# Three small moves in a one-core trunk layer: where one row of weights is loaded, which buffers hold the gate values, which PSUM bank holds the context state

## The chip, the cores and the metric

The kernel runs on one core of a Trainium2 chip. The metric is the device time of one execution in microseconds (us). Engines are named as the profile names them: PE is TensorE (PEld its weight load), DVE is VectorE, ACT is ScalarE, POOL is GpSimd, SP is SyncE, which here only issues DMAs. A q behind a name (ACTq, SPq) is that engine's instruction queue, whose instructions run in order.

## The reference, cut to what matters

One trunk layer over 512 latent tokens of width 1024, with a 256-token context prefix, in float32:

```
h    = rms_norm(x)*(1+scale)+shift ;  proj = h @ w_in
xbc  = silu(depthwise_conv4(proj[x,B,C]))                    # 8 groups of 4 heads
h0   = final SSD state of the context, forward and backward   # context only
y    = ssd_scan(forward, h0_f) + rev(ssd_scan(backward, h0_b)) + d_skip*xs
       # per 128-token chunk: y_diag + (C . state entering the chunk) * exp(la)
ssm  = group_rms_norm(y * silu(z)) @ w_out_ssm
conf = (silu(layer_norm(conv31(glu))) * silu(proj[cg])) @ w_out_conf
out  = (sigmoid(g1)*ssm + sigmoid(g2)*conf) @ w_out
x    = rms_norm(x + gate*out) * final_norm_w
```

## The kernel before, in words

Every big product is done in three float32r passes (high part by high part, high by low, low by high), 128 columns of weights at a time. A weight block of 128 x 1024 comes by DMA into `raw` (two buffers, on the SP queue), ACT copies it to `whi` (L168), DVE subtracts to get `wlo` (L169), and PE uses both; `whi` and `wlo` have three buffers each.

The order of the instructions on each engine is not the order of the program text. A planner sorts them: on each engine it takes, of the instructions whose inputs and buffers are free by its own estimate, the one that stands first in the program (`high_priority` ones, such as L168, L169 and `evac`, ahead). The engines then run this fixed order, and wait on semaphores where the real times differ from the estimates.

The stages that the change touches:

- **Eight groups** (L462 on). Per group: projections, conv, then the context state: two products into `cp` (L539), which ACT copies to `s0` (`evac`, L174). Then three state sums for the chunks, each a pair of products into a `cp` tile (L547), which DVE adds to the decayed state before it (L549, L551). `s0` and the three sums are the states entering the chunks; the carried-over outputs are products of these states with `cT` into `yo` (L586). All `cp` tiles take turns with the transposes and `sps` in the two banks of tag `m`; `yo` takes two banks of its own, one tile at a time. The order of the tiles in `m` is: context `cp`, first, second, third chunk's `cp`, then `sps`. With two banks, the second chunk's `cp` takes the bank of the context `cp`, and the third chunk's that of the first. The `yo` tile of a group is read by DVE (L591) before the next group begins.
- **The SSM output product** (L706 on, eight steps d of 48 matmuls). In steps 2 to 5 of the program text, two channel blocks k a step are turned into the conformer's input: transposes, a SiLU (L725), the product with the stored gate values `zcl` (L720 loads them from DRAM on the ACT queue, L726 multiplies), and the split into `vhi` and `vlo`. `zcl` has one buffer, tag `cr`. DVE also adds up the residual gate from `mg` blocks (L703), which go through `raw` like the weights. The result of step d is stored to DRAM on the ACT queue (L730).
- **The last products** (pool `fp`, L739 on). For each d: the conformer output product (24 matmuls, blocks `wc` on the SP queue), and the preparation of one block of `w_out`: it is loaded on the ACT queue into `rawo` (L146, two buffers), multiplied by the gate (L750), and split into `wh` and `wl`. DVE merges the two branches into `mg` (L761, L762, with `t2` and `m1b` loaded on the ACT queue), which is split into `mhi` and `mlo`. Then the last product (L777) runs over all d. `fnb`, the final norm's weights spread over 128 partitions (512 KB written), is loaded ahead of this loop on the ACT queue (L745) and first read at L780.

The pool `fp` lies where the pools `lnp` and `yp` lay. In bytes of a partition from their common start: `lnp` takes 16,896, `yhi` and `ylo` 32,768 each, so `t1` lies at 82,432 to 98,816, the two `gt` buffers (with `sv`) behind it to 102,912, and then `up`. In `fp`, `wh`, `wl`, `mhi` and `mlo` take 98,304, so `fnb` lies at 98,304 to 102,400 and the first `rawo` buffer at 102,400 to 106,496. So `fnb` overlaps the end of `t1`, whose last block is read by the last store of L730; `rawo` doesn't, it overlaps `gt` and `up`. A tile waits only for the tiles under it.

Of the kernel before, what the change touches and what calls it, by code (L numbers as in the profile page):

```python
# [8 lines left out]
F32 = mybir.dt.float32  # L9
# [6 lines left out]
P = 128  # L16
D = 1024
KO = D // P
L = 512
# [3 lines left out]
R = 4  # L23
# [57 lines left out]
def hybrid_block(ctx: ExitStack, tc: tile.TileContext, x, cx, pack, wmod, bgate, wall, fnw, out):  # L81
    nc = tc.nc
# [15 lines left out]
    def pv(name):  # L98
        o, w = OFF[name]
        return pk[:, o:o + w]  # L100
# [34 lines left out]
    def follow(ins, prev):  # L135
        tc.add_manual_dep(ins.ins, prev.ins.name,
                          mybir.DependencyInfo(mybir.DependencyClass.NoSync, mybir.DependencyReason.DATA),
                          reason="activation table order")
# [37 lines left out]
    def split(dst_hi, dst_lo, src):  # L176
        S.copy(dst_hi, src)
        V.tensor_sub(dst_lo, src, dst_hi.bitcast(F32))

    def log_exp_table(after):  # L180
        t = S.preload_act_table_set("natural_log_exp_and_others")
        follow(t, after)
        return t
# [107 lines left out]
    def acc_tile():  # L291
        pxn[0] += 1
        tag = pxt[pxn[0] % len(pxt)]
        return pp.tile([P, L], F32, name="px", tag=tag, bufs=2 if tag == "px" else 1)
# [60 lines left out]
    if True:  # L355
        pp_stack = ctx
        pp = pp_stack.enter_context(tc.tile_pool(name="pp", bufs=1, space=PSUM, reuse_waits="tile"))
# [65 lines left out]
        with tc.tile_pool(name="sp", bufs=1, reuse_waits="tile") as sp:  # L423
# [38 lines left out]
            for g in range(NG):  # L462
# [70 lines left out]
                        wend[:, d0:d1, c, h0:h0 + R].unsqueeze(3).broadcast_to([P, nd, R, 64]))  # L533
                    return w
                sts = []
                cp = pp.tile([P, 2, R, 64], F32, name="cp", tag="m", bufs=2)
                for i in range(NCC):
                    w = xw(NCH + i, 0, 2)
                    T.matmul(cp, btok[:, NCH + i], w, start=(i == 0), stop=(i == NCC - 1))  # L539
# [3 lines left out]
                for i in range(NCH - 1):  # L543
                    cp = pp.tile([P, 2, R, 64], F32, name="cp", tag="m", bufs=2)
# [29 lines left out]
                for t in range(2):  # L574
                    yd = pp.tile([P, L], F32, name="yd", tag="yd", bufs=1)
                    for c in range(NCH):
                        for hf in range(2):
                            r = 2 * t + hf
                            T.matmul(yd[hf * 64:(hf + 1) * 64, c * P:(c + 1) * P],  # L579
                                     xtok[:, c, t, hf * 64:(hf + 1) * 64], mixes[c][:, r], start=True, stop=True)  # L580
                    yo = pp.tile([P, 2, L], F32, name="yo", tag="yo", bufs=1)
# [33 lines left out]
        yp = ypool_stack.enter_context(tc.tile_pool(name="yp", bufs=1, reuse_waits="tile"))  # L615
# [3 lines left out]
        def gemm3(ps, d, rhi, rlo, between):  # L619
            i = 0  # L620
            for kind in ("ws0", "ws1"):
                hi, lo = wblock(kind, d)
                for k in range(KO):
                    T.matmul(ps, hi[:, k, :], rhi[:, i], start=(i == 0), stop=False)  # L624
                    T.matmul(ps, hi[:, k, :], rlo[:, i], start=False, stop=False)  # L625
                    T.matmul(ps, lo[:, k, :], rhi[:, i], start=False, stop=(i == 2 * KO - 1))  # L626
                    i += 1
                if kind == "ws0":
                    between()
# [5 lines left out]
        def to_tokens_all():  # L635
            while ready:
                to_tokens(*ready.pop(0))
# [12 lines left out]
        for i in range(KO - ne):  # L650
            up, _ = conv_in(yp, pp, ne + i)
            taps.append(conv_taps(yp, ne + i, up, lambda d, a: ready.append((d, a))))
            if i == 0:
# [6 lines left out]
                    for g in range(NG):  # L660
                        rb = yp.tile([P, L], F32, name="rb", tag="rb", bufs=2)
                        nc.scalar.dma_start(out=rb, in_=rs_d[g].rearrange("c l -> (c l)").unsqueeze(0).broadcast_to([P, L]))
                        for t in range(2):
                            jj = 2 * g + t
                            yl = yp.tile([P, L], F32, name="yl", tag="yl", bufs=2)
# [3 lines left out]
            for k in (2 * i, 2 * i + 1):  # L669
                pg, _ = proj(pp, "cg", k)  # L670
                zc = yp.tile([P, L], F32, name="zc", tag="gt", bufs=GT[0])
# [12 lines left out]
            if i < ne:  # L684
                cr = yp.tile([P, L], F32, name="cr", tag="cr", bufs=1)
# [15 lines left out]
        def gate(i):  # L701
            raw = wraw("mg", i)
            V.scalar_tensor_tensor(out=ga.rearrange("p n c -> p (n c)"), in0=raw, scalar=scg[:, i:i + 1],  # L703
                                   in1=ga.rearrange("p n c -> p (n c)"), op0=ALU.mult, op1=ALU.add)

        for d in range(KO):  # L706
            po = pp.tile([P, 2, L], F32, name="po", tag="yo", bufs=1)[:, 0] if d % 2 else pp.tile([P, L], F32, name="po", tag="yd", bufs=1)
            gemm3(po, d, yhi, ylo, lambda: gate(d))
            if d == 0:
                to_tokens_all()  # L710
                mv = yp.tile([P, NCH, 2], F32, name="mv")
                for t in range(NCH):
                    V.bn_aggr(out=mv[:, t], in_=bst[:, t])
                rl = rsqrt_small(yp, "rl", mv[:, :, 1], 1.0)
                for t in range(NCH):
                    V.tensor_scalar(ln[:, t], ln[:, t], mv[:, t, 0:1], rl[:, t:t + 1], op0=ALU.subtract, op1=ALU.mult)
            if 2 <= d <= 5:
                for k in (2 * d - 4, 2 * d - 3):
                    zc = yp.tile([P, L], F32, name="zcl", tag="cr", bufs=1)
                    nc.scalar.dma_start(out=zc, in_=cg_d[k])  # L720
                    tp = pp.tile([P, NCH, P], F32, name="tpb", tag="m", bufs=2)
                    for t in range(NCH):
                        T.transpose(tp[:, t], ln[:, t, k * P:(k + 1) * P], ident)
                    sv = yp.tile([P, L], F32, name="sv", tag="gt", bufs=GT[0])
                    last = S.activation(sv, tp.rearrange("p t c -> p (t c)"), AF.Silu, scale=pv("lnw")[:, k:k + 1], bias=pv("lnb")[:, k:k + 1])  # L725
                    V.tensor_mul(sv, sv, zc)  # L726
                    split(vhi[:, k], vlo[:, k], sv)
            with tc.high_priority():
                V.scalar_tensor_tensor(out=t1[:, d], in0=t1[:, d], scalar=1.0, in1=po, op0=ALU.add, op1=ALU.mult)
            nc.scalar.dma_start(out=m1d[d], in_=t1[:, d])  # L730
# [8 lines left out]
    with tc.tile_pool(name="fp", bufs=1, reuse_waits="tile") as fp:  # L739
        wh = fp.tile([P, KO, D], F32R, name="wh")  # L740
        wl = fp.tile([P, KO, D], F32R, name="wl")
        mhi = fp.tile([P, KO, L], F32R, name="mhi")
        mlo = fp.tile([P, KO, L], F32R, name="mlo")
        fnb = fp.tile([P, D], F32, name="fnb")
        nc.scalar.dma_start(out=fnb, in_=fnw.broadcast_to([P, D]))  # L745
        for d in range(KO):
            po = acc_tile()
            hi, lo = wblock("wc", d)
            raw = wraw("wo", d, fp, "rawo", 2, nc.scalar)
            V.tensor_mul(raw, raw, gb.rearrange("p n c -> p (n c)"))  # L750
            split(wh[:, d], wl[:, d], raw)
            for k in range(KO):
                T.matmul(po, hi[:, k, :], vhi[:, k], start=(k == 0), stop=False)
                T.matmul(po, hi[:, k, :], vlo[:, k], start=False, stop=False)
                T.matmul(po, lo[:, k, :], vhi[:, k], start=False, stop=(k == KO - 1))
            t2 = fp.tile([P, L], F32, name="t2", tag="t2", bufs=2)
            nc.scalar.dma_start(out=t2, in_=t2d[d])
            m1 = fp.tile([P, L], F32, name="m1b", tag="m1b", bufs=1)
            nc.scalar.dma_start(out=m1, in_=m1d[d])
            mg = t2  # L760
            V.scalar_tensor_tensor(out=mg, in0=t2, scalar=1.0, in1=po, op0=ALU.add, op1=ALU.mult)  # L761
            V.tensor_add(mg, mg, m1)  # L762
            split(mhi[:, d], mlo[:, d], mg)
        table = log_exp_table(last)
        for t in range(NCH):
            cs = slice(t * P, (t + 1) * P)
            xr = fp.tile([P, D], F32, name="xr", tag="xr", bufs=1)
            nc.scalar.dma_start(out=xr, in_=x[cs, :])
            o = fp.tile([P, D], F32, name="o", tag="o", bufs=2)
            parts = ((0, 512), (512, 512)) if t < NCH - 1 else ((0, 512), (512, 256), (768, 256))  # L770
            s2 = fp.tile([P, 3], F32, name="s2", tag="s2", bufs=2)[:, 0:len(parts)]
            for n, (c0, cn) in enumerate(parts):
                ns = slice(c0, c0 + cn)
                po = acc_tile()[:, 0:cn]
                for k in range(KO):
                    for st_, rh, a, b in ((mhi, wh, True, False), (mhi, wl, False, False), (mlo, wh, False, True)):
                        T.matmul(po, st_[:, k, cs], rh[:, k, ns], start=(a and k == 0), stop=(b and k == KO - 1))  # L777
                V.tensor_add(o[:, ns], po, xr[:, ns])
                S.activation(xr[:, ns], o[:, ns], AF.Square, accum_out=s2[:, n:n + 1])
                V.tensor_mul(o[:, ns], o[:, ns], fnb[:, ns])  # L780
            sm = fp.tile([P, 1], F32, name="sm", tag="sm", bufs=2)
            V.tensor_reduce(sm, s2, axis=mybir.AxisListType.X, op=ALU.add)
            r = rsqrt_small(fp, "rf", sm, 1.0 / D, table)
            S.mul(o[:, 0:512], o[:, 0:512], r)
            nc.sync.dma_start(out=out[cs, 0:512], in_=o[:, 0:512])
            V.tensor_scalar(o[:, 512:D], o[:, 512:D], r, None, op0=ALU.mult)
            nc.scalar.dma_start(out=out[cs, 512:D], in_=o[:, 512:D])
# [75 lines left out]
```

## Time and profile before

| | |
|---|---|
| time, three runs | 945.36 us median (943.8 to 948.3) |
| time of the profiled execution | 943.96 us |
| its span, first to last instruction | 941.9 us (2.06 us lie around it) |
| PE busy | 911.8 us, 97% of the span |
| DVE busy, ACT busy | 734.2 us (78%), 522.8 us (56%) |
| granted TensorE clock, mean | 0.995 |

Busy time is the time in which an engine has an instruction under way. Matmuls overlap, so two of them start some 0.23 us apart though each lasts 0.39. The time that counts is what is lost between the starts of PE's matmuls.

### The profile page before, as it was taken

What the parts mean: (1) busy time and instruction counts of PE and PEld (TensorE: products, weight loads), DVE (VectorE), ACT (ScalarE), POOL (GpSimd) and SP (SyncE); (2) the same over time, 40 slices, a digit from 0 to 9 for tenths busy, and PEclk for the clock granted to TensorE, in tenths of its full rate; (3) what the DMA queues carried; (4) which work ended last, traced back from release to release, by engine and by line L of the source; (5) the groups of instructions that cost most, each with busy time, mean ns of one, the idle gap of its engine ahead of it and who ended that gap; (6) DMA issues with size and microseconds to landing.
All of it is one profiled execution on the core that took longest, in us unless ns stands there. A gap on an engine that the chain in (4) does not pass through costs nothing.

```text
span 941.9 us, 12605 instructions
## 1 busy us (share of the span) xinstructions
PE 911.8 (97%) x4647; PEld 730.7 (78%) x4647; DVE 734.2 (78%) x1232; ACT 522.8 (56%) x926; POOL 10.1 (1%) x117
## 2 busy tenths in 40 slices
PE   6999999999999999999999999999999999999896
PEld 1287788788788788787887887788888888868686
DVE  1577499997699994899993999889999965448833
ACT  4638846767667668468477567454433234323322
POOL 0000000000000000000000000000000000000000
PEclk9999999999999999999999999999999999999999
DMA  9424512522422324225125122356633356568522
GB/s 378 193 87 140 180 45 84 173 58 97 149 68 98 119 92 158 73 68 180 44 90 179 34 79 79 131 204 215 212 112 132 114 179 205 152 180 267 190 78 79
DMA packets 41375, 127.04 MB, mean 135 GB/s; under 512 B 4546, under 2 KB 4962, under 8 KB 40291
## 3 DMA queue, kind: packets, MB, share of 16 engines
q1 hardware_dynamic: 25040, 93.22, 29.8%
q10 hardware_dynamic: 16274, 33.04, 10.3%
q8 instruction: 36, 0.59, 0.3%
q14 instruction: 25, 0.20, 0.1%
HBM read 112.46 MB, written 13.78 MB: 134 GB/s over the span
## 4 chain that ended last, share of the span: by engine, by line
PE 71%; ACT 11%; DMA 9%; DVE 5%; issue 3%; SPq 0%; ACTq 0%; DVEq 0%
PE px L344 14%; PE px L343 14%; PE px L350 14%; DMA raw<-in_wall 6%; PE px L777 4%; PE yo L586 3%; PE mp L262 3%; ACT el L508 3%; PE pc L346 3%; PE pc L347 2%; PE pc L352 2%; ACT whi L168 2%; PE yd L579 2%; PE cp L547 2%; ACT e L510 2%
## 5 line engine op out<-in xcount | busy, mean ns | idle before, releaser
L343 PE MATMUL px<-hx,whi 128*128 128x512 f32 x712 | 284.5, 400 | 1.4 <-ACT pad L174 1.4
L344 PE MATMUL px<-hx,whi 128*128 128x512 f32 x712 | 281.5, 395 | 0.0
L350 PE MATMUL px<-hx,wlo 128*128 128x512 f32 x704 | 277.0, 393 | 0.0
L169 DVE TENSOR_TENSOR wlo<-raw,whi 128x1024 fp32r<-128x1024 f32 x112 | 137.3, 1226 | 67.8 <-ACT whi L168 67.1
L168 ACT CAST whi<-raw 128x1024 fp32r<-128x1024 f32 x112 | 117.7, 1051 | 130.1 <-PE px L344 62.7
L327 DVE SCALAR_TENSOR_TENSOR ac<-up,pk,ac 128x512 f32<-128x512 f32 x232 | 162.8, 756 | 0.0
L343 PEld LDWEIGHTS px<-hx,whi 128*128 128x128 f32 x712 | 133.9, 188 | 28.9 <-ACT pad L174 1.8
L344 PEld LDWEIGHTS px<-hx,whi 128*128 128x128 f32 x712 | 133.9, 188 | 23.7 <-issue 3.1
L350 PEld LDWEIGHTS px<-hx,wlo 128*128 128x128 f32 x704 | 132.4, 188 | 22.1 <-issue 0.7
L568 ACT ACTIVATE tm<-slm,dtT 128x128 f32<-128x128 f32 x128 | 40.7, 393 | 53.8 <-DVE slm L560 45.2
L495 ACT ACTIVATE e<-la,laN 128x128 f32<-128x128 f32 x128 | 40.3, 394 | 37.0 <-PE yd L579 35.4
L346 PE MATMUL pc<-hc,whi 128*128 128x256 f32 x200 | 57.1, 286 | 0.2 <-ACT pad L174 0.2
L347 PE MATMUL pc<-hc,whi 128*128 128x256 f32 x200 | 56.7, 284 | 0.0
L352 PE MATMUL pc<-hc,wlo 128*128 128x256 f32 x192 | 54.5, 284 | 0.0
L626 PE MATMUL po<-yhi,wlo 128*128 128x512 f32 x128 | 50.1, 392 | 2.3 <-DVE wlo L169 2.3
L440 DVE SCALAR_TENSOR_TENSOR xsT<-pad,pk,xsT 128x771 f32<-128x771 f32 x48 | 48.9, 1019 | 2.6 <-ACT xsT L438 2.5
L624 PE MATMUL po<-yhi,whi 128*128 128x512 f32 x128 | 50.4, 394 | 0.0
L625 PE MATMUL po<-ylo,whi 128*128 128x512 f32 x128 | 49.8, 389 | 0.0
L346 PEld LDWEIGHTS pc<-hc,whi 128*128 128x128 f32 x200 | 37.7, 188 | 7.5 <-issue 0.7
L347 PEld LDWEIGHTS pc<-hc,whi 128*128 128x128 f32 x200 | 37.6, 188 | 6.5
L508 ACT ACTIVATE el<-la 64x512 f32<-64x512 f32 x64 | 40.1, 627 | 0.5
L262 PE MATMUL mp<-wm,scf 128*4 128x512 f32 x64 | 31.7, 631 | 6.4 <-DMA wm<-in_wmod 6.4
(274 smaller groups left out, 1415.9 us busy)
## 6 DMA issues: line engine op xcount, KB each, us to landing
raw<-in_wall SPq DMA_DIRECT2D x121, 512.0 KB, 3.3
la<-la_d SPq DMA_DIRECT2D x32, 512.0 KB, 4.3
wm<-in_wmod SPq DMA_DIRECT2D x8, 1024.0 KB, 13.7
y_d<-y ACTq DMA_DIRECT2D x16, 256.0 KB, 2.2
yl<-y_d ACTq DMA_DIRECT2D x16, 256.0 KB, 3.3
raw<-in_wall ACTq DMA_DIRECT2D x8, 512.0 KB, 4.3
xt<-in_x SPq DMA_DIRECT2D x2, 1024.0 KB, 10.1
t_d<-t ACTq DMA_DIRECT2D x8, 256.0 KB, 2.0
```

Source lines behind the costliest of these rows:

```text
L168: S.copy(hi, raw)
L169: V.tensor_sub(lo, raw, hi.bitcast(F32))
L262: T.matmul(mp, scf[:, k + j].rearrange("p a b -> p (a b)"), wm[:, k + j], start=(k + j == 0), stop=(k + j == KO - 1))
L327: V.scalar_tensor_tensor(out=a, in0=up[:, :, t:t + GRID], scalar=cwh[:, d, t:t + 1], in1=a, op0=ALU.mult, op1=ALU.add)
L343: T.matmul(px, hi[:, k, :], hx[0][:, k, :], start=first, stop=False)
L344: T.matmul(px, hi[:, k, :], hx[1][:, k, :], start=False, stop=last and lo is None)
L346: T.matmul(pc, hi[:, k, :], hc[0][:, k, :], start=first, stop=False)
L347: T.matmul(pc, hi[:, k, :], hc[1][:, k, :], start=False, stop=last and lo is None)
L350: T.matmul(px, lo[:, k, :], hx[0][:, k, :], start=False, stop=last)
L352: T.matmul(pc, lo[:, k, :], hc[0][:, k, :], start=False, stop=last)
L508: S.activation(el[hf * 64:(hf + 1) * 64, :, :, c * P:(c + 1) * P], las[c][hf * 64:(hf + 1) * 64].rearrange("p d (t h) l -> p d t h l", h=2 ...
L624: T.matmul(ps, hi[:, k, :], rhi[:, i], start=(i == 0), stop=False)
```

## The change

Three edits. The context state's `cp` is now the first bank of a `yo` tile, no longer one of the `m` tiles. `zcl` uses the tag `yl` (two buffers, in use at L665 before this stage), no longer `cr` (one buffer). The load of `fnb` stands behind step 4 of the last loop and goes on the SP queue, no longer ahead of the loop on the ACT queue.

```diff
-                cp = pp.tile([P, 2, R, 64], F32, name="cp", tag="m", bufs=2)
+                cp = pp.tile([P, 2, L], F32, name="cp", tag="yo", bufs=1)[:, 0].rearrange("p (d r q) -> p d r q", d=2, r=R)
                 for i in range(NCC):
                     w = xw(NCH + i, 0, 2)
                     T.matmul(cp, btok[:, NCH + i], w, start=(i == 0), stop=(i == NCC - 1))
...
                 for k in (2 * d - 4, 2 * d - 3):
-                    zc = yp.tile([P, L], F32, name="zcl", tag="cr", bufs=1)
+                    zc = yp.tile([P, L], F32, name="zcl", tag="yl", bufs=2)
                     nc.scalar.dma_start(out=zc, in_=cg_d[k])
...
         fnb = fp.tile([P, D], F32, name="fnb")
-        nc.scalar.dma_start(out=fnb, in_=fnw.broadcast_to([P, D]))
         for d in range(KO):
...
             split(mhi[:, d], mlo[:, d], mg)
+            if d == 4:
+                nc.sync.dma_start(out=fnb, in_=fnw.broadcast_to([P, D]))
```

## Rows read from the trace of the kernel before

**Rows 1.** The page, part 1: busy us, share of the span, instructions.

```profile
PE 911.8 (97%) x4647; PEld 730.7 (78%) x4647; DVE 734.2 (78%) x1232; ACT 522.8 (56%) x926; POOL 10.1 (1%) x117
```

**Rows 2.** Waits of PE: waited for, us in total, times, longest.

```profile
PE mp L262 <- DMA wm<-in_wmod: 6.4, 1, 6.4
PE cp L547 <- ACT s L174: 5.9, 7, 2.2
PE px L777 <- ACT mhi L177: 3.6, 2, 2.1
PE po L626 <- DVE wlo L169: 2.3, 2, 1.7
```

**Rows 3.** Timeline of the second group: start, us, engine, line, [idle before <-releaser].

```profile
181.08 0.57 ACT L174 COPY s<-cp 128x512 f32<-128x512 f32 x1
...
181.70 1.13 PE L547 MATMUL cp<-xw,btok 128*128 128x256 f32 x4 [0.65 <-ACT s L174]
...
182.67 0.38 PE L586 MATMUL yo<-cT,s 128*128 128x128 f32 x2
...
182.78 0.68 DVE L551 TENSOR_TENSOR sn<-sn,cp 128x512 f32<-128x512 f32 x1
...
183.72 1.02 PE L547 MATMUL cp<-xw,btok 128*128 128x256 f32 x4
...
184.40 0.58 PE L343 MATMUL px<-hx,whi 128*128 128x512 f32 x1
...
184.81 0.40 PE L344 MATMUL px<-hx,whi 128*128 128x512 f32 x1
```

**Rows 4.** Timeline, 816 to 834 us: DVE and PE in the SSM output product.

```profile
816.60 0.69 DVE L726 TENSOR_TENSOR sv<-sv,zcl 128x512 f32<-128x512 f32 x1 [4.09 <-DMA zcl<-cg_d]
817.21 1.22 DVE L169 TENSOR_TENSOR wlo<-raw,whi 128x1024 fp32r<-128x1024 f32 x1
...
823.18 1.28 DVE L703 SCALAR_TENSOR_TENSOR ga<-raw,scg,ga 128x1024 f32<-128x1024 f32 x1 [3.55 <-DMA raw<-in_wall]
...
825.66 0.50 PE L626 MATMUL po<-yhi,wlo 128*128 128x512 f32 x1 [0.59 <-DVE wlo L169]
...
831.26 0.69 DVE L726 TENSOR_TENSOR sv<-sv,zcl 128x512 f32<-128x512 f32 x1 [3.68 <-DMA zcl<-cg_d]
831.87 1.22 DVE L169 TENSOR_TENSOR wlo<-raw,whi 128x1024 fp32r<-128x1024 f32 x1
...
833.14 0.50 PE L626 MATMUL po<-yhi,wlo 128*128 128x512 f32 x1 [1.71 <-DVE wlo L169]
```

**Rows 5.** Timeline, 820 to 853 us: ACT, its queue, and DVE.

```profile
820.27 1.28 ACT L181 ACT_TABLE_LOAD   x1
...
840.11 0.33 ACTq L730 DMA_DIRECT2D m_d<-t  x1
...
843.56 0.34 ACTq L745 DMA_DIRECT2D fnb<-in_fnw  x1
844.00 0.39 ACTq L146 DMA_DIRECT2D raw<-in_wall  x1
...
852.06 1.23 DVE L750 TENSOR_TENSOR raw<-raw,gb 128x1024 f32<-128x1024 f32 x1 [8.47 <-DMA raw<-in_wall]
```

**Rows 6.** Windows: length, busy us (count) of PE PEld DVE ACT POOL, clock, DMA.

```profile
843.60:852.06 8.46, 8.46 (x39) 6.98 (x39) 0.00 (x0) 1.05 (x1) 0.00 (x0) 1.00 0.87 273
852.06:894.25 42.19, 38.58 (x166) 30.82 (x165) 39.40 (x45) 17.54 (x20) 0.00 (x0) 0.97 0.68 218
...
893.20:898.50 5.30, 5.29 (x12) 4.13 (x13) 2.43 (x4) 0.72 (x2) 0.00 (x0) 0.50 0.00 0
898.50:903.80 5.30, 5.30 (x25) 4.35 (x24) 1.29 (x2) 0.73 (x2) 0.00 (x0) 1.00 0.00 0
```

**Rows 7.** The page, part 6: DMA issues, KB each, median us to landing.

```profile
raw<-in_wall ACTq DMA_DIRECT2D x8, 512.0 KB, 4.3
```

**Rows 8.** Line L753, PE's matmuls: ns min/median/max, first and last start.

```profile
L753 PE MATMUL px<-vhi,whi x64: 389/389/798, 839.6 to 883.0; 128*128 128x512 f32 x64
```

## The prediction

> **What bounds the kernel now.** The page comes first: PE is busy for 97% of the span [rows 1], the other engines far less, so time can be won only where PE stands still or runs slowly. Next the waits of PE alone [rows 2]. The reader should see that there are few of them and that three touch the three edits: 5.9 us in front of the state sums L547 (seven waits for ACT's copy of the context state), 3.6 us in front of the last product L777 (two waits for `mhi`), and 2.3 us in the SSM output product (two waits for `wlo`). The largest, 6.4 us for the first modulation weights, isn't touched. Then each place is opened in the timeline, to see what ended last [rows 3 to 5], and the tail in windows [rows 6]: there the reader should see that after the two waits for `mhi` the granted clock stands at 0.50, so 1.2 GHz instead of 2.4, for some 5 us. That is time lost by PE which no list of waits shows.
>
> **The context state in the bank of `yo`.** Nothing is added or dropped: the same two products, the same copy. What is dropped is one dependence: the second chunk's `cp` no longer needs the bank that ACT empties. In the second group that pair began at 181.70, 0.05 after the copy's end (181.08 + 0.57), having waited 0.65 [rows 3]. But two other things hang on the same copy. The first carried-over product L586 reads `s0` itself; it now runs at 182.67, right behind the pair. And the third chunk's `cp` takes the bank of the first one, free when L551 ends (182.78 + 0.68 = 183.46); it starts at 183.72, 0.26 later [rows 3], and L551 stands in a chain that begins with `s0`. The planner puts PE's work where it believes the copy is done. The pair moves forward, projection matmuls fill the place behind it, and L586, then the first thing in line that wants `s0`, moves to where the pair stood: the real copy is late by the same amount there, so PE waits 0.65 in front of L586 instead. I cost the edit at 0. It holds the new bank no longer than needed, since `yo` can't start before `s0` is there anyway, and the `yo` of the group before is long read. What is unknown is the new order. Below: all 5.9 us of [rows 2] go. Above: the first projection matmul after such products starts its successor 0.41 us on (184.40 to 184.81 [rows 3]), where two matmuls usually stand 0.21 apart (25 in 5.30 us [rows 6]); two more such breaks in each of eight groups cost 16 x 0.2 = 3.2. The value 0 is nearer to the upper end, because the row shows both successors of the copy following within 2 us.
>
> **`zcl` in two buffers.** With one buffer the next load can start only when the product L726 before it is done, so DVE stands 4.09 and 3.68 us for it [rows 4]. Behind it in DVE's order is L169, the split of the next weight block. At 831.26 the load has landed, L726 takes 0.69, L169 runs at 831.87, and PE, which waits for that `wlo`, resumes at 833.14 after 1.71 idle [rows 4]. The other wait is one step further away: L169 at 817.21 came after a 4.09 wait for `zcl`; only then was its `raw` buffer free for the next `mg` block, DVE stood 3.55 for that block's landing at 823.18, and PE stood 0.59 before 825.66 [rows 4]. The tag `yl` was last used before this stage, so two loads can be there before the first L726, and each later one has a whole pair of blocks ahead of it: at one pair a step of 48 matmuls (48 x 0.21, some 10 us) against waits of 4, both DVE waits go, and with them the 2.3 us of PE [rows 2]. I take -2.3. Bounds: 0, if DVE still stands for the `mg` block (3.55 [rows 4]), and -2.3, as there is no more to get. The number of DMAs and bytes is as before; the loads are only earlier, under a busy PE.
>
> **`fnb` off the ACT queue.** This is the largest term. ACT's queue runs in order: the store of the last SSM step goes out at 840.11, `fnb` only at 843.56, the first block of `w_out` at 844.00 [rows 5]. `fnb` lies over the end of `t1`, so it must wait until that store has read it; `rawo` doesn't lie there. So `fnb` holds up the block behind it for over 3 us, and then 512 KB of it go ahead on the same queue: the block is there at 852.06, 8.1 us after its issue [rows 5], against a median of 4.3 [rows 7]. DVE does nothing at all from 843.6 to 852.06, then works 39.40 of 42.19 us until the last `mlo` [rows 6]. This stretch is paced by DVE, and PE catches up with it at its end: the two waits for `mhi`, 3.6 us [rows 2], and then the halved clock, 12 matmuls begun in 5.30 us against 25 in the next 5.30 [rows 6], so 13 x 0.212 = 2.8 us. Without `fnb` on the queue the block can go out right behind the store, at 840.5, and be there 4.3 later [rows 7], at 844.8: 7.2 us sooner. Some of that may be lost on the weight copies; 3.6 us are enough for both waits to go. What is late next: the conformer product ends at 883.4 [rows 8]; two merges and a copy of some 0.7 each (as L726 [rows 4]) put the last `mhi` at 885.5, and PE would ask for it at 893.2 - 3.6 = 889.6 [rows 6, 2]. So I take 3.6 + 2.8 = 6.4 off. Bounds: 0 and -6.4.
>
> On its new queue `fnb` probably isn't late at all: the planner takes what is free, as it took the last table load at 820.27 [rows 5], though its line stands behind the whole last loop. So I expect it on SP near 843.5, when the store has landed. Behind it on SP wait only weight blocks that need a `raw` buffer, and DVE frees none between 843.6 and 852.06 [rows 6]; nobody waits for that. Its one added issue costs ACT nothing and SP is idle.
>
> Here a rule speaks against the edit. In [rows 5] the block took 8.1 us behind `fnb`. The Trainium skill (DMA: Bandwidth & Descriptors, Issuing engines are not separate DMA queues) says that DMAs issued from the scalar and sync queues run on the same 16 engines and interleave, so that another queue saves only issue time. By that rule the transfer of the block is no shorter, and the tail gains only what the earlier issue gives: issued at 840.5 and 8.1 long it lands at 848.6, 3.5 us sooner, which is 6.3 instead of 6.4. What decides is whether the block is issued ahead of `fnb`.
>
> **The sum.** -2.3 - 6.4 + 0 = -8.7, on the profiled execution's 943.96 us (941.9 of span and 2.06 around it): 935.3. That execution is 1.4 below the median of the runs shown, which would give 936.7. I say 936.0.
>
> **Rivals.**
> 1. *The context wait really goes.* Then PE doesn't stop for the copy anywhere: another 5.9 off, 929.4. For it: the waits are short (0.65) and the pair that moves ahead takes 1.1 us. Against: the chain through L551 has 0.26 to spare. Chance 0.12.
> 2. *`fnb` isn't what delays the block.* If `fp` opens for all its tiles at once, the block is issued at 843.5 on its queue while `fnb` goes on the other, shares the engines and lands 8.1 us later, at 851.6; the tail gains 0.5. Only the 2.3 stay: 941.2. The Trainium skill's rule above speaks for this. With the tail won and the 2.3 not, it is 937.6, inside the main case. Against: 840.11 + 0.33 leaves the ACT queue empty for 3 us [rows 5]. Chance 0.15.
> 3. *The change doesn't do what it says.* The loads are only relabelled and the planner's new order puts other stalls in place of these: 943 to 945. Chance 0.11.
> 4. *Slower: the bank of `yo`.* `yo` has one tile at a time. If the planner puts L586 close behind the context products, PE stands in every group for the copy with nothing to fill it. The longest such wait today is 2.2 [rows 2]; at 2.4 a group, 8 x 2.4 - 5.9 = 13.3 more, the gains are gone and 0.5% is lost; at 2.7 it is 951. For it: ACT's copy is late whenever ACT is behind. Against: six of the seven waits share 3.7 us, 0.6 each. Chance 0.07.
>
> **How the numbers follow.** The main case, 932.5 to 939, has 0.55. The range 929 to 943 takes in the upper half of rival 1's spread, all of rival 2 and the lower edge of rival 3, and leaves out some 0.19. No change means within 0.5% of 945.36, which is 940.6 to 950.1, about what a measurement can tell. Below it are the main case, rival 1 and half of rival 2: 0.75. Within: the rest of rival 2 and rival 3: 0.18. Above: 0.07.
>
> **What would show it.** In the profile after: no wait of PE for `mhi` in front of L777, and the clock at 1.00 through the last product; the first L750 before 847; no DVE wait for `zcl`, and no PE wait for `wlo` in L624 to L626; the waits for ACT's copy under L586 or L547, some 5 us in all. `fnb` on SP near 843 less what is gained before. I am wrong if the first L750 still comes 8 us after DVE falls idle, or if new waits of PE over 1 us stand in the eight groups.

## The result, and the profile after

The changed kernel takes 933.88 us (median of 4 runs, 933.09 to 934.34) against 944.58 for the kernel before on the same chip: ratio 0.9879 (95% interval 0.985 to 0.9909), so some 11 us faster. Predicted were 936.0 us, range 929 to 943. Measured again on another chip, the same kernel had a ratio of 0.9899 (0.9875 to 0.9923). The profiled execution took 934.34 us with a span of 932.6, against 943.96 and 941.9: 9.3 us of span are gone. (In the changed kernel the lines behind L745 count one less, and from the new load of `fnb` on one more: L749 there is L750 before, L778 is L777.)

The waits of PE, first lines of the view (waited for, us in total, times, longest), answer to [rows 2]:

```profile
PE mp L262 <- DMA wm<-in_wmod: 6.5, 1, 6.5
PE yo L586 <- ACT s L174: 4.9, 7, 1.6
PE hp L280 <- ACT xt L240: 1.8, 1, 1.8
```

The wait for the copy of the context state has moved from L547 to L586. It still occurs seven times and is 1.0 us smaller. The waits for `mhi` (3.6 us) and for `wlo` (2.3 us) are not in the view any more. The second group in the timeline, against [rows 3]:

```profile
180.56 0.70 PE L547 MATMUL cp<-xw,btok 128*128 128x256 f32 x2
181.25 0.57 ACT L174 COPY s<-cp 128x512 f32<-128x512 f32 x1
...
181.87 0.49 PE L586 MATMUL yo<-cT,s 128*128 128x128 f32 x2 [0.38 <-ACT s L174]
...
182.78 0.40 PE L343 MATMUL px<-hx,whi 128*128 128x512 f32 x1
...
184.54 1.03 PE L547 MATMUL cp<-xw,btok 128*128 128x256 f32 x4
```

The pair of L547 no longer waits; it runs before the copy, and L586 stands 0.05 us behind the copy's end (181.25 + 0.57), where the pair stood before. PE waits 0.38 there instead of 0.65.

DVE, ACT's queue and SP's queue in the SSM output product and behind it, against [rows 4, 5]:

```profile
804.63 1.29 DVE L703 SCALAR_TENSOR_TENSOR ga<-raw,scg,ga 128x1024 f32<-128x1024 f32 x1 [2.31 <-DMA raw<-in_wall]
805.84 1.22 DVE L169 TENSOR_TENSOR wlo<-raw,whi 128x1024 fp32r<-128x1024 f32 x1
806.97 1.29 DVE L726 TENSOR_TENSOR sv<-sv,zcl 128x512 f32<-128x512 f32 x2
...
815.04 1.29 DVE L703 SCALAR_TENSOR_TENSOR ga<-raw,scg,ga 128x1024 f32<-128x1024 f32 x1 [0.95 <-DMA raw<-in_wall]
...
817.38 1.29 DVE L726 TENSOR_TENSOR sv<-sv,zcl 128x512 f32<-128x512 f32 x2
...
836.78 0.33 ACTq L730 DMA_DIRECT2D m_d<-t  x1
...
837.20 0.39 ACTq L146 DMA_DIRECT2D raw<-in_wall  x1
...
839.17 0.33 SPq L764 DMA_DIRECT2D fnb<-in_fnw  x1
841.17 1.23 DVE L749 TENSOR_TENSOR raw<-raw,gb 128x1024 f32<-128x1024 f32 x1 [1.80 <-DMA raw<-in_wall]
```

Both products of a pair now run back to back (x2) with no wait for `zcl`. Two pairs stand 10.4 us apart (806.97 to 817.38), where the second products stood 14.7 apart (816.60 to 831.26 [rows 4]). `fnb` goes out 2.4 us behind the store (3.45 before), now on SP, and the first block of `w_out` has gone ahead of it, 0.42 behind the store. The first product with the gate is at 841.17 instead of 852.06 [rows 5]. The tail in windows (columns as in [rows 6]) is full and at the full clock:

```profile
881.00:893.00 12.00, 12.00 (x55) 9.93 (x54) 6.93 (x9) 2.57 (x6) 0.00 (x0) 1.00 0.09 22
893.00:905.00 12.00, 12.00 (x55) 9.93 (x54) 4.56 (x12) 3.22 (x9) 0.00 (x0) 1.00 0.25 89
```

By place the account closes: 1.0 (copy) + 2.3 (`wlo`) + 3.6 (`mhi`) + some 2.5 (halved clock) = 9.4, against 9.3 of span. Which edit earned which part is another question, and there the prediction was wrong.

### The profile page after: what moved, and what is told of

Same layout as the page of the kernel before. It is cut to its first block, busy times and chain, and to the rows that moved or that the text cites. A ratio compares the mean times of both kernels' runs of the same rounds, so it can differ in the third digit from the quotient of the medians.

```text
span 932.6 us, 12628 instructions
## 1 busy us (share of the span) xinstructions
PE 909.4 (98%) x4647; PEld 729.5 (78%) x4647; DVE 734.0 (79%) x1232; ACT 522.2 (56%) x926; POOL 10.1 (1%) x117
## 4 chain that ended last, share of the span: by engine, by line
PE 85%; ACT 10%; DMA 2%; issue 1%; DVE 1%; SPq 0%; ACTq 0%
PE px L344 15%; PE px L343 15%; PE px L350 14%; PE px L778 5%; PE yo L586 3%; PE po L624 3%; PE po L626 3%; PE po L625 3%; PE mp L262 3%; PE pc L346 3%; PE pc L347 2%; PE pc L352 2%; ACT el L508 2%; PE yd L579 2%; ACT whi L168 2%; PE px L754 2%
## 5 line engine op out<-in xcount | busy, mean ns | idle before, releaser
L169 DVE TENSOR_TENSOR wlo<-raw,whi 128x1024 fp32r<-128x1024 f32 x112 | 136.9, 1222 | 69.6 <-ACT whi L168 69.3
```

The source lines that it names most:

```text
L169: V.tensor_sub(lo, raw, hi.bitcast(F32))
```

## Experiments

**Each edit alone, and the two without the context edit** (one chip; the kernel before has a median of 945.04 there).

`only_cp`:

```diff
-                cp = pp.tile([P, 2, R, 64], F32, name="cp", tag="m", bufs=2)
+                cp = pp.tile([P, 2, L], F32, name="cp", tag="yo", bufs=1)[:, 0].rearrange("p (d r q) -> p d r q", d=2, r=R)
```

> Only the first edit: the context state's sum goes into the bank of yo; gate values and norm weights as before. Theory (the wait is moved, not removed): PE waits as long for ACT's copy, now in front of L586; 0 to -1 us, ratio to before 0.999 to 1.000. Rival (the wait really goes): 4 to 6 us less, ratio 0.994 to 0.996. Rival (the new order costs breaks): up to 3 us more, ratio 1.003.

942.80 us, ratio 0.9976 (0.996 to 0.9993): some 2.3 us faster, not 0. Its waits of PE:

```profile
PE yo L586 <- ACT s L174: 5.5, 7, 1.5
PE px L777 <- ACT mhi L177: 3.5, 2, 1.8
...
PE po L626 <- DVE wlo L169: 1.7, 1, 1.7
```

The wait moves to L586, and the waits at the two other places stay, as they should.

`only_zcl`:

```diff
-                    zc = yp.tile([P, L], F32, name="zcl", tag="cr", bufs=1)
+                    zc = yp.tile([P, L], F32, name="zcl", tag="yl", bufs=2)
```

> Only the second edit: gate values in two buffers. Theory: both waits of PE for wlo in the SSM output product go, 2.3 to 2.6 us less, ratio 0.997 to 0.998; the waits for mhi in front of the last product and the halved clock stay. Rival (DVE still stands for the mg block and PE behind it): no change. Rival (an earlier finish of this stage also lets the last stage start sooner): more than 3 us less.

937.81 us, ratio 0.9925 (0.9896 to 0.9953): 7.1 us faster, three times what the prediction gave this edit. `fnb` is where it was, and yet the tail is nearly won: one wait for `mhi` is left, of 0.5 us, and none for `wlo`. The gain lies in these two stages and not in an earlier start of the last one: the conformer product begins at 840.2 here and at 839.6 before, and from there to the end of the span it takes 95.9 us instead of 102.3. (The groups took longer in this execution; the section on the prediction says why.)

```profile
PE cp L547 <- ACT s L174: 7.4, 7, 2.0
...
PE px L777 <- ACT mhi L177: 0.5, 1, 0.5
```

The timeline of this kernel, to be held against [rows 5]:

```profile
839.80 0.33 ACTq L730 DMA_DIRECT2D m_d<-t  x1
...
841.85 0.34 ACTq L745 DMA_DIRECT2D fnb<-in_fnw  x1
842.23 0.45 ACTq L146 DMA_DIRECT2D raw<-in_wall  x1
...
848.05 1.23 DVE L750 TENSOR_TENSOR raw<-raw,gb 128x1024 f32<-128x1024 f32 x1 [5.66 <-DMA raw<-in_wall]
```

From the store to `fnb` it takes 2.05 us instead of 3.45, from the block's issue to the product 5.82 instead of 8.06; together 3.6 us sooner behind the store. The last two columns of the windows (DMA share and GB/s) show why, first of the kernel before:

```profile
830.00:834.00 4.00, 2.29 (x11) 1.56 (x10) 2.74 (x4) 1.57 (x2) 0.00 (x0) 1.00 0.03 10
834.00:838.00 4.00, 4.00 (x19) 3.30 (x18) 1.76 (x3) 1.06 (x1) 0.00 (x0) 1.00 0.87 257
838.00:842.00 4.00, 4.00 (x16) 2.64 (x15) 2.32 (x3) 1.05 (x1) 0.00 (x0) 1.00 0.65 225
```

and then of `only_zcl`:

```profile
830.00:834.00 4.00, 4.00 (x19) 3.30 (x18) 0.32 (x1) 0.55 (x1) 0.00 (x0) 1.00 0.70 231
834.00:838.00 4.00, 4.00 (x20) 3.30 (x19) 1.23 (x1) 0.50 (x1) 0.00 (x0) 1.00 0.30 109
838.00:842.00 4.00, 4.00 (x16) 2.63 (x15) 2.72 (x4) 1.04 (x1) 0.00 (x0) 1.00 0.24 94
```

Before, while DVE waits for the last `zcl`, no `raw` buffer comes free and the DMA engines stand still (0.03). The weight blocks that should have moved then move from 834 on, and are in the way of the store, of `fnb` and of the first block of `w_out`. With two buffers they move before 834. The other profiles agree: from the issue of the last store to that of `fnb`, which waits for it, it takes 2.9 to 3.6 us in the four with one buffer (before, `only_cp`, `only_fnb`, `no_zcl`) and 2.05 to 2.4 in the seven with two.

The edit also changes the tile's place in memory and, through the planner, the order of DVE and ACT; no run separates these from the second buffer.

`only_fnb`:

```diff
-        nc.scalar.dma_start(out=fnb, in_=fnw.broadcast_to([P, D]))
...
+            if d == 4:
+                nc.sync.dma_start(out=fnb, in_=fnw.broadcast_to([P, D]))
```

> Only the third edit: the norm weights on the SP queue. Theory: the first block of w_out is issued right behind the last store, its product L749 starts some 7 us sooner, the two waits for mhi and the halved clock go: 6.4 to 6.7 us less, ratio 0.993; the two waits for wlo (2.3 us) stay. Rival (the bytes, not the order, delay the block): the first L749 still comes 8 us after DVE falls idle and less than 1 us is gained.

941.83 us, ratio 0.9966 (0.9945 to 0.9988): 3.2 us faster, half of what the prediction gave it. The waits for `mhi` are gone, as predicted; but PE waits longer one stage earlier:

```profile
PE cp L547 <- ACT s L174: 6.2, 7, 2.4
PE po L626 <- DVE wlo L169: 5.8, 3, 2.3
```

The order on PE and DVE is that of the kernel before up to the end of this stage, so 5.8 instead of 2.3 isn't the edit's work: the wait for a late `wlo` differs from execution to execution (`first_alone` below, with the same order, has 3.9). The profiled execution, 944.53 us, is also the slowest of the twelve (937.1 to 944.5). And behind the last of the three waits (2.30, up to 839.18) the clock falls here too, to a mean of 0.65 over the next 4.9 us:

```profile
836.49:839.20 2.71, 0.41 (x3) 0.03 (x1) 1.91 (x3) 1.18 (x2) 0.00 (x0) 1.00 0.01 3
839.20:844.07 4.87, 4.87 (x14) 3.88 (x15) 2.67 (x4) 1.43 (x2) 0.00 (x0) 0.65 0.74 256
```

`no_cp` (`zcl` and `fnb`, the last two diffs together):

> The second and third edit without the first. Theory: the same as the whole change within 1 us, ratio to before 0.989 to 0.991, and PE's waits for ACT's copy stand in front of L547 again, 5 to 6 us. Rival (the first edit carries part of the gain): 3 to 5 us slower than the whole change, ratio 0.992 to 0.994.

935.09 us, ratio 0.9895 (0.9867 to 0.9922), which is 2.7 us below `only_zcl`, with overlapping intervals. No wait for `wlo` or `mhi`; the copy's wait is under L547, 7.7 us.

**Where `fnb` stands, with the other two edits in place** (another chip, before 943.49). Four variants of the changed kernel. `fnb_first`, where `fnb` no longer lies over `t1` and goes out on the ACT queue ahead of the loop:

```diff
     with tc.tile_pool(name="fp", bufs=1, reuse_waits="tile") as fp:
+        fnb = fp.tile([P, D], F32, name="fnb")
...
-        fnb = fp.tile([P, D], F32, name="fnb")
+        nc.scalar.dma_start(out=fnb, in_=fnw.broadcast_to([P, D]))
...
-            if d == 4:
-                nc.sync.dma_start(out=fnb, in_=fnw.broadcast_to([P, D]))
```

> The whole change, but fnb's tile stands first in its pool, so that it no longer lies over t1, and its load is on the ACT queue ahead of the loop, as before. It needn't wait for the store, but its 512 KB may stand in front of the first block of w_out on the same queue. Theory A (fnb did harm by waiting for the store and holding the queue meanwhile): the load goes out long before the store, the first product with the gate comes as early after the start of the conformer product as in the whole change (some 1 to 2 us after it, bound 3), no wait for mhi over 0.5 us, ratio to before 0.988, within 2 us of the whole change. Theory B (the bytes on the same queue do it): the block takes over 7 us from issue to landing, waits for mhi of 1 to 3.6 us and the halved clock behind them return, 3 to 6 us slower than the whole change, ratio 0.991 to 0.995. Theory C (with two buffers for zcl the place of fnb hardly matters any more, as context edit plus zcl alone already took the tail's waits): within 1.5 us of the whole change whatever the transfer takes.

`fnb_act_late`:

```diff
             if d == 4:
-                nc.sync.dma_start(out=fnb, in_=fnw.broadcast_to([P, D]))
+                nc.scalar.dma_start(out=fnb, in_=fnw.broadcast_to([P, D]))
```

> The whole change, but the load of fnb, still behind step 4 of the last loop, goes on the ACT queue. Theory A (what counts is that the first block of w_out is issued ahead of fnb; the queue is of no account): as the whole change within 1 us, ratio 0.988, no wait for mhi over 0.5 us. Theory B (the other queue is what helps): fnb delays a later block of w_out or the loads of t2 and m1b by its 4 to 7 us, some wait for mhi of 1 to 3 us returns, ratio 0.990 to 0.993.

`fnb_x3`:

```diff
                 nc.sync.dma_start(out=fnb, in_=fnw.broadcast_to([P, D]))
+                for _ in range(2):
+                    more = fp.tile([P, D], F32, name="more", tag="o", bufs=2)
+                    nc.sync.dma_start(out=more, in_=fnw.broadcast_to([P, D]))
```

> The whole change with two more loads of the same row (512 KB each) right behind fnb on SP, into tiles that nothing reads before they are used for the output: 1 MB more for the DMA engines in the tail. Theory A (order: a load beside the blocks costs the tail nothing as long as it stands in no queue ahead of them): ratio within 0.001 of the whole change (0.988), first product with the gate no more than 1 us later. Theory B (bytes: fnb's transfer shares the engines with the blocks and that is what it costs): each 512 KB costs what fnb cost, 2 to 4 us a load, waits for mhi return, ratio 0.992 to 0.996.

934.67 us (0.9907, 0.9875 to 0.9939), 935.68 (0.991, 0.9875 to 0.9944) and 934.62 (0.9906, 0.9877 to 0.9935): no difference between them that can be measured, and none has a wait for `wlo` or `mhi`. In `fnb_act_late` the load goes out only at 863.2. In `fnb_first` it goes out right behind the store's issue, and the first product with the gate comes 6.6 us after the first matmul of the conformer product (843.0 - 836.4), against 4.0 in the changed kernel (841.2 - 837.2) and 12.5 before (852.1 - 839.6): the bytes ahead of the block on its queue do delay it, by some 2.6 us, and PE doesn't wait for it. In `fnb_x3` three loads go out on SP (start, us, queue, line):

```profile
838.02 0.33 SPq L764 DMA_DIRECT2D fnb<-in_fnw  x1
838.40 1.00 SPq L767 DMA_DIRECT2D more<-in_fnw  x2
839.86 1.23 DVE L749 TENSOR_TENSOR raw<-raw,gb 128x1024 f32<-128x1024 f32 x1 [1.59 <-DMA raw<-in_wall]
```

A further 1 MB behind the first block costs no time that can be measured. So of the theories laid down for these three, the one that the place of `fnb` hardly matters once `zcl` has two buffers is the one that fits all of them. The Trainium skill (DMA: Bandwidth & Descriptors, Issuing engines are not separate DMA queues) says that DMAs from either queue run on the same engines and interleave, so that the choice of queue saves only issue time. These times, the same on either queue, agree, but with the slack that the tail has here they would hardly show a difference.

`cp_dve` was tried for the largest wait that is left:

```diff
-                evac(s0, cp)
+                with tc.high_priority():
+                    V.tensor_copy(s0, cp)
```

> The whole change, but the context state is copied from its bank to s0 by DVE (ahead of its other work), not by ACT. The whole change still loses 4.9 us in front of the first carried-over product, seven waits for ACT's copy. Theory A (the copy is late because ACT is behind): these waits go, 3 to 5 us faster than the whole change, ratio 0.983 to 0.985. Theory B (the planner puts the product where it believes the copy done, and DVE, busy for 78% of the span, is behind as often): PE waits as long or longer for DVE, 0 to 4 us slower, ratio 0.988 to 0.992.

935.39 us, ratio 0.9905 (0.9869 to 0.9941): no gain. The wait only changes its releaser:

```profile
PE yo L587 <- DVE s L542: 4.4, 3, 2.0
```

**One edit taken out, and `fnb` placed elsewhere with nothing else changed** (a third chip, before 942.81; the whole change there, `whole_again`, 932.95).

> The whole change once more, beside the three others on one chip, as the measure for them: ratio 0.988 to 0.991 by what was measured; waits for the copy of the context state 4 to 5 us, no wait for wlo or mhi over 0.5 us. Were one of these waits to come back here, it would vary from one execution to the next and couldn't be charged to an edit.

No wait for `wlo` or `mhi`, 4.4 us for the copy.

`no_fnb` (the whole change, with `fnb` loaded as before):

```diff
         fnb = fp.tile([P, D], F32, name="fnb")
+        nc.scalar.dma_start(out=fnb, in_=fnw.broadcast_to([P, D]))
...
-            if d == 4:
-                nc.sync.dma_start(out=fnb, in_=fnw.broadcast_to([P, D]))
```

> The edits to the context state and to zcl, with fnb loaded ahead of the loop on the ACT queue, as before: the whole change less fnb. Theory A (with zcl in two buffers the tail has its slack whatever fnb does; fnb and zcl win the same few us twice): first product with the gate still 5 to 8 us after DVE falls idle, but waits for mhi under 0.7 us, within 2 us of the whole change, ratio 0.988 to 0.992. Theory B (the effects add up; fnb gives 3 us of its own): 3 us slower than the whole change, ratio 0.992 to 0.995, waits for mhi of 1 to 3 us.

934.26 us, ratio 0.9914 (0.9892 to 0.9936), so 1.3 us more than the whole change, with overlapping intervals. Its timeline still shows `fnb` holding the queue until the store has landed, and DVE idle for the block:

```profile
836.44 0.33 ACTq L730 DMA_DIRECT2D m_d<-t  x1
...
838.50 0.34 ACTq L745 DMA_DIRECT2D fnb<-in_fnw  x1
838.88 0.45 ACTq L146 DMA_DIRECT2D raw<-in_wall  x1
...
844.74 1.22 DVE L750 TENSOR_TENSOR raw<-raw,gb 128x1024 f32<-128x1024 f32 x1 [5.70 <-DMA raw<-in_wall]
```

PE waits for none of it: the tail has enough slack, as theory A had it.

`no_zcl` (the whole change, with `zcl` as before):

```diff
-                    zc = yp.tile([P, L], F32, name="zcl", tag="yl", bufs=2)
+                    zc = yp.tile([P, L], F32, name="zcl", tag="cr", bufs=1)
```

> The edits to the context state and to fnb, with zcl in one buffer: the whole change less zcl. Theory A (the late zcl sets the pace of DVE through four pairs of blocks, and its 3 to 6 us at the end of the SSM product are lost there, before the tail, whatever becomes of fnb): waits of 2 to 6 us for wlo in the SSM output product, none for mhi, 5 to 8 us slower than the whole change, ratio 0.993 to 0.997. Theory B (the prediction's sizes: zcl 2.3, fnb 6.4): 2 to 3 us slower than the whole change, ratio 0.990 to 0.991.

937.51 us, ratio 0.9945 (0.9926 to 0.9964): 4.6 us more than the whole change by the medians. The ratio is that of theory A, the place isn't. With `fnb` on SP and the first block of `w_out` issued ahead of it, the tail still waits:

```profile
PE yo L586 <- ACT s L174: 4.4, 7, 1.5
PE px L778 <- ACT mhi L177: 2.6, 1, 2.6
...
PE po L626 <- DVE wlo L169: 0.9, 1, 0.9
```

The block is used 6.1 us after its issue here (838.56 to 844.66), against 4.0 in the changed kernel, though `fnb` isn't ahead of it: with one buffer it is late by itself. But in `no_fnb` its product comes later still behind the first matmul of the conformer product (7.9 us against 7.1 here), and PE doesn't wait there. So the first block alone doesn't explain the 2.6 us; what does is open.

`first_alone` (the kernel before, with `fnb`'s tile first in its pool; the order of instructions on PE, DVE, ACT and SP is the same as before):

```diff
     with tc.tile_pool(name="fp", bufs=1, reuse_waits="tile") as fp:
+        fnb = fp.tile([P, D], F32, name="fnb")
...
-        fnb = fp.tile([P, D], F32, name="fnb")
         nc.scalar.dma_start(out=fnb, in_=fnw.broadcast_to([P, D]))
```

> The kernel before, and only fnb's tile placed first in its pool, so that it no longer lies over t1; still loaded on the ACT queue ahead of the loop, zcl in one buffer. Theory A (fnb's harm was that it waited for the store and held the queue): as the move of fnb alone, ratio 0.9966 within 0.002, the first product with the gate under 6 us after DVE falls idle, no waits for mhi over 1 us. Theory B (the harm is in 512 KB ahead of the block on one queue): no gain, ratio 0.999 to 1.001, waits for mhi of 2 to 4 us and the halved clock as before.

939.54 us, ratio 0.9965 (0.9947 to 0.9983): as much as the move to SP alone. The load goes out 0.36 behind the store's issue, not 3.45:

```profile
843.23 0.33 ACTq L730 DMA_DIRECT2D m_d<-t  x1
843.59 0.46 ACTq L745 DMA_DIRECT2D fnb<-in_fnw  x1
844.16 0.47 ACTq L146 DMA_DIRECT2D raw<-in_wall  x1
```

So what `fnb` did to the kernel before was to hold the queue while it waited for the store. Its bytes ahead of the block still make it late (7.0 us from issue to product, 844.16 to 851.13, against 4.0 in `only_fnb`), but in time the two kernels can't be told apart; each ratio is known to some 2 us.

## Why the prediction was right, and where its steps were not

Read across the profiles, the losses of PE sort by one edit. Waits for `wlo` and for `mhi`, us, of one execution each:

| kernel | `zcl` buffers | `fnb` | `wlo` | `mhi` |
|---|---|---|---|---|
| before | 1 | waits for the store, ACT | 2.3 | 3.6 |
| `only_cp` | 1 | the same | 1.7 | 3.5 |
| `first_alone` | 1 | not over `t1`, ACT | 3.9 | 0.2 |
| `only_fnb` | 1 | SP | 5.8 | 0 |
| `no_zcl` | 1 | SP | 0.9 | 2.6 |
| `only_zcl` | 2 | waits for the store, ACT | 0 | 0.5 |
| `no_fnb` | 2 | the same | 0 | 0 |
| the change, and the six others | 2 | off ACT's head or not over `t1` | 0 | 0 |

With one buffer 3.5 to 5.9 us are lost, in the one place or the other, wherever `fnb` is; with two, 0.5 at most.

The lengths of the two stages say more. From the first matmul of the SSM output product to the first of the conformer product it takes 92.5 us in all nine profiles with two buffers, and 93.7 to 101.1 in the five with one. From there to PE's last matmul it takes 94.7 before, 94.8 in `only_cp`, 91.3 in `no_zcl`, and 87.6 to 88.5 in the other eleven. So either edit alone wins the tail in its profile (87.7 in `only_fnb`, 88.4 in `only_zcl`, 87.6 with both); but while `zcl` has one buffer, time is lost before the tail (101.1 in `only_fnb`).

**The sum** of -8.7 us was right: -9.3 by the spans, and by the time 2.1 us more than forecast. By place this was no luck, as the waits for `wlo` and `mhi` and the halved clock went as forecast; by edit it was, as the three terms were each off and their errors partly cancel. The main case came true, and its signs: the waits for the copy under L586, 4.9 us; no DVE wait for `zcl`; the first product with the gate before 847, 4.0 us behind its block's issue (4.3 predicted); `fnb` on SP when the store has landed, though its line stands behind step 4; the clock at 1.00 to the end. One sign of being wrong showed too: a new wait over 1 us in the groups. L586 waits 1.6 us in the third group, where L547 waited 0.45 before; over all groups the wait still fell.

**The terms were mis-sized.** The step that failed is the bound of `zcl`, "-2.3, as there is no more to get", and with it the whole 6.4 us of the tail put down to `fnb` alone, though either edit wins them. `zcl` measured 7.1 us alone and 4.6 as the last edit added. The prediction saw that a late `zcl` kept back L169 and the `raw` buffer, and counted only the waits of PE in that stage. It did not follow the kept-back weight blocks into the tail, where they crowd the store and the first block of `w_out`. The DMA share of 0.03 from 830 to 834, where weights were wanted, would have said so. The halved clock was put at 2.8 us, from 25 matmuls in a window of 5.30; that count takes in some under way at its edges. In the timeline they start 0.23 apart at the full clock, so the 12 at the halved one lost some 2.5.

`fnb` measured 3.2 us alone against 6.4. The mechanism was as described (`first_alone` shows that it was the wait for the store), and in the profile of `only_fnb` the tail is 7.0 us shorter; but the one buffer took part of it back in the stage before. With `zcl` in two buffers between 1.3 and 2.7 us are left of it, which these runs don't tell from nothing, and the profile of `no_fnb` has no wait that it could come from.

**The context edit** measured 2.3 us alone against 0. That the wait would move to L586 was right, that it would be as long (0.65 in the second group) was not: it is 0.38 there. In the five profiles without this edit it is 5.9, 7.4, 6.2, 7.7 and 6.7 us (mean 6.8), in the eight with it and ACT's copy 5.5, 4.9, 4.2, 4.4, 4.3, 3.8, 4.5 and 4.4 (mean 4.5): 2.3 less, the same as by the time. Of these, 0.9 us are the same in every profile: in the second, fourth, sixth and eighth group the wait is 0.50 to 0.66 without the edit and 0.36 to 0.38 with it. The copy ends as late as ever there, 4.6 us after the first context product in both; PE does the pair that used to wait before the copy ends, so it has less time left to wait. The rest comes from the third, fifth and seventh group, where the wait goes from 0.45 to 2.41 without the edit and from 0.2 to 1.6 with it, from profile to profile; why is open.

The list of waits leaves out a part. Behind the longest of these waits the granted clock fell to 0.50 in three of the five profiles without the edit (`only_zcl`, `no_cp`, `only_fnb`), which makes the group 1.5 us longer (6.1 instead of 4.6 from the copy's end to the group's first `sps` matmul); in the nine with it, it never did. First `only_zcl`, seventh group, the line of the timeline and the window behind it (columns as in [rows 6], 0.60 on the mean of these 4 us), then the same of the kernel before, where the clock stayed at 1.00:

```profile
516.62 1.37 PE L547 MATMUL cp<-xw,btok 128*128 128x256 f32 x4 [1.98 <-ACT s L174]
```

```profile
516.60:520.60 4.00, 3.98 (x14) 3.34 (x15) 4.00 (x9) 0.00 (x0) 0.00 (x0) 0.60 0.42 131
```

```profile
514.54 1.15 PE L547 MATMUL cp<-xw,btok 128*128 128x256 f32 x4 [2.23 <-ACT s L174]
```

```profile
514.50:518.50 4.00, 3.96 (x21) 3.30 (x22) 4.00 (x9) 0.00 (x0) 0.00 (x0) 1.00 0.43 131
```

Shorter waits may thus save clock as well; five profiles against nine don't prove it. In all, the first matmul of the SSM output product comes at 744.1 to 747.8 us in the five (mean 746.3) and at 742.5 to 744.6 in the eight (mean 743.9). Added to the other two edits (0.9895 without it, 0.9879 and 0.9899 with it) its gain isn't resolved.

The singles add up to 12.6 us, the whole gives 9.5 to 11.4. With singles known to some 2 us each, that difference isn't clear of the noise; that `zcl` and `fnb` feed the same slack shows in the tail, which each wins alone. **Rival 1** fell: the wait for the copy didn't go. **Rival 2** fell as stated, since the block goes out 0.42 us behind the store's issue, but has a core of truth: with `zcl` mended, `fnb` isn't what delays PE. **Rivals 3 and 4** fell.

Open: why the waits for `wlo` with one buffer range from 0.9 to 5.8 us in nearly the same program, what makes `mhi` late in `no_zcl`, and what `fnb` still gives. No variant beats the change.

## What to carry to other kernels

A wait of an engine that isn't the bottleneck is to be followed through the buffers that it keeps occupied, up to the next stage: here a stretch with idle DMA engines (0.03 busy for 4 us), just before a stage that loads much, was paid for in that stage. When two edits feed the same slack, price them by taking each one out of the whole and by doing each one alone; the waits in one profile tell where time is lost, not which edit will win it, and what varies from execution to execution needs more than one profile. A load that waits for memory to come free holds all that stands behind it on its queue (here for 3.45 us), so give it memory that is free, or let the urgent load go first.

## What the runs showed of the hardware

- The clock after waits of PE. How long a wait is doesn't decide alone. Behind single waits of 1.98, 2.07 and 2.41 us in the groups (`only_zcl`, `no_cp`, `only_fnb`) the granted clock fell to 0.50, so 1.2 GHz instead of 2.4; behind one of 2.23 in the kernel before it stayed at 1.00, and in `no_zcl` behind one of 2.61 us, up to 889.19, too:

```profile
886.10:889.20 3.10, 0.49 (x3) 0.18 (x2) 3.06 (x4) 1.66 (x2) 0.00 (x0) 1.00 0.18 64
889.20:894.20 5.00, 4.89 (x19) 3.64 (x20) 2.40 (x4) 0.72 (x2) 0.00 (x0) 1.00 0.00 0
```

  In `only_cp` it stood at 0.50 from 893.9 to 897.9, behind two waits of 1.8 us each, the second up to 893.9; [rows 6] show the same after two waits of 1.5 and 2.1.
- Loads issued behind it did not slow the load that mattered: in `fnb_x3` the two added ones took 9.8 us each (median), while the first block of `w_out`, issued 1.9 us ahead of `fnb` and 2.3 ahead of the added loads, was used 3.8 us after its issue, against 4.0 in the changed kernel.
